# Low weight halves of an output product written by an accumulating transfer instead of a subtract

## The chip, the cores and the metric

The kernel runs on one core of a Trainium2 chip. Its time is the device time of one execution in microseconds (us). Engines: TensorE (PE, with its weight load PEld), VectorE (DVE), ScalarE (ACT), GpSimd (POOL) and SyncE (SP), each with its own instruction stream that runs in order; transfers are issued by an engine's queue and carried out by 16 DMA engines.

## The reference

Two layers of a transformer block over 256 tokens and 256 context tokens, model width 2048, branch width 4096, all float32. Layer 0 mixes tokens by a Fourier transform, layer 1 by windowed attention. Cut to what matters here:

```python
def _fourier_branch(h, w_in, w_mix):
    u, z = jnp.split(h @ w_in, 2, axis=-1)
    ...
    f = jnp.einsum('bngc,gcd->bngd', f, w_mix).reshape(b, n, D_BRANCH)
    return f * jax.nn.silu(z)

def reference(...):
    for i in range(DEPTH):
        ...
        x = x + gate * (y @ w_out[i])
        if need_ctx:
            xc = xc + gate_c * (yc @ w_out[i])
    return _rmsnorm(x, final_g)
```

The change touches `y @ w_out[0]` and `yc @ w_out[0]`, layer 0's output product.

## The kernel before, in words

**Precision.** [...] So every float32 operand is split in two fp32r tiles: a high half h (a rounded copy, ACT, L60) and a low half l = src - h (a subtract, DVE, L61). `mm3` (L72 to L75) forms a product with three matmuls, high times high (L73), high times low (L74) and low weights times high data (L75).

**Layout.** Both token sets lie side by side, 512 columns. A matmul has a 128x128 block of weights and 128x512 data. The branch result y is 32 tiles of 128x512 (`ys`), one for 128 branch channels.

**The changed loop** (L646 to L665) runs over 32 iterations i, in two sweeps `sw` of 1024 output channels each, so that the sweep's results fill the eight PSUM banks `o[0..7]`. In a sweep `kg` runs over 16 weight tiles of 128x2048 (1 MB). A weight tile holds two halves j of 128x1024, each for one tile of y, with eight blocks b of 128 output channels: 2 x 8 x 3 = 48 matmuls. `raw` (L43 to L47) loads a weight tile by SP's queue into one of three buffers, `ws_split` (L69) splits both halves (`half_split`, L63 to L67) into tiles of the pool `ws`, which has six buffers of 128x1024. `y_split0` (L624) splits the two y tiles of the next iteration into `act` tiles (34 buffers).

**What else runs there.** `ada_jobs` (L530 to L553) is a generator that computes layer 1's modulation vectors on DVE, from weight tiles of the same three `raw` buffers (`in_adw`), at about one tile an iteration; its lines are L545 (multiply and sum) and L535 (POOL loads `cb`). From kg = 12 on, POOL's queue loads two blocks of the input x each iteration (L656), into which `evac0` (L630 to L641) adds the gated result of each PSUM bank (L634, DVE) and sums squares (L637 ACT, L639 DVE) for the next norm, at kg = 15. In the first and the last kg of a sweep (`edge`) the matmuls go through the banks b on the outside and the halves j on the inside; else j is outside.

**Around it.** Ahead of the loop, the last of the z products ends: its result goes through a Silu on ACT into one of two z tiles (L583) and is multiplied into y on DVE (L584). The pools of that part are closed and their memory is used again. After the loop come transposes (L674, L680), the norm's sums (L691, which needs the last L639), then `rsqrt` (L81, L85) and a broadcast by L99, and layer 1's first product, whose weights are already being split (its `wl` subtracts stand among the last evacuations on DVE).

**Order.** The program is written in this order of lines, but a list scheduler decides the place of each instruction in its engine's stream from its own estimate of times; a tile pool with n buffers makes the write of use k wait for the last reader of use k - n.

The norm's sums after the loop:

```python
    for t in range(4):
        for i in range(2):
            PE.matmul(o[:, t : t + 1], sqs[i][:, t * P : (t + 1) * P], ones[:, 0:1], start=i == 0, stop=i == 1)   # L691
    r4 = rsqrt(const, o[:, 0:4], 4, "q")
```

## Time and profile before

| | |
|---|---|
| time, median of 3 runs | 1863.13 us (1860.94 to 1863.33) |
| the profiled execution | 1861.45 us |
| its span in the trace | 1859.1 us |
| mean granted TensorE clock | 0.995 of full |
| bytes read from HBM | 353.10 MB |
| DMA issues of the changed stage | `in_wo` 32 of 1024 KB, `in_adw` 64 of 1024 KB (some before it), `in_xT` 16 of 256 KB |

The profile lists, for the one profiled execution, busy times by engine, a chain of waits followed back from the last instruction, groups of instructions with the same line and tiles (busy time in all, mean in ns, idle time of the engine just before them and what ended it), and DMA issues with the time from issue to landing. A timeline row reads: start in us, duration, engine, line, operation, output tile <- input tiles, shapes, count, and in brackets the idle time before it with its releaser. Matmuls are pipelined, so a matmul's duration is longer than the distance between two starts. "PE ps L691 <- DVE act L639" reads: PE at line 691 waited for DVE's line 639 to write the tile.

### The profile page before, as it was taken

How to read it: one execution, taken by the hardware profiler on the slowest of the kernel's cores; microseconds unless marked ns; L12 is line 12 of the kernel's file. 1: busy time of each engine (PE TensorE's matmuls, PEld its weight loads, DVE VectorE, ACT ScalarE, POOL GpSimd, SP SyncE). 2: the span in 40 equal slices, each digit the busy share in tenths (PEclk: the TensorE clock that was granted, in tenths of full speed). 3: DMA queues.
4: the chain of work that ended last, by engine and by line, in shares of the span. 5: the costliest groups of instructions: out<-in, count | busy, mean ns of one | idle time of the engine just before them, and what ended most of it. 6: DMA issues, size and time to landing. Idle time of an engine off the chain costs nothing.

```text
span 1859.1 us, 26469 instructions
## 1 busy us (share of the span) xinstructions
PE 1817.6 (98%) x9889; PEld 1549.3 (83%) x9889; DVE 1389.6 (75%) x2766; ACT 954.6 (51%) x1657; POOL 176.8 (10%) x189
## 2 busy tenths in 40 slices
PE   6899999999999999999999999999999999999997
PEld 4579999888888888888888787888888888887886
DVE  4669888786868788687974825888878878887455
ACT  5444444432222243224322624888888888896343
POOL 0011111100000000000000001111220220300001
PEclk9899999999999999999999999999999999999999
DMA  9999888666656647763675323333333333434543
GB/s 395 407 296 246 246 220 242 228 226 244 224 212 234 227 172 264 264 236 131 226 286 204 114 92 143 128 136 126 124 115 135 136 115 135 159 137 179 186 178 136
DMA packets 76127, 367.39 MB, mean 198 GB/s; under 512 B 23200, under 2 KB 23344, under 8 KB 40928
## 3 DMA queue, kind: packets, MB, share of 16 engines
q1 hardware_dynamic: 49104, 324.83, 47.3%
q0 software_dynamic: 22320, 33.15, 7.1%
q10 hardware_dynamic: 4576, 7.74, 1.3%
q8 instruction: 77, 1.26, 0.3%
q14 instruction: 50, 0.41, 0.1%
HBM read 353.10 MB, written 12.59 MB: 197 GB/s over the span
## 4 chain that ended last, share of the span: by engine, by line
PE 90%; DMA 4%; DVE 3%; ACT 2%; issue 1%; POOL 0%; ACTq 0%; POOLq 0%; SPq 0%; DVEq 0%
PE ps L74 23%; PE ps L73 23%; PE ps L75 23%; PE ps L910 6%; PE ps L912 3%; DMA raw<-in_awp 3%; PE ps L966 3%; PE ps L981 2%; PE ps L980 2%; PE ps L946 2%; PE ps L947 2%; DMA raw<-in_wu 1%; PE ps L208 1%; PE ps L829 0%; DVE wl L61 0%
## 5 line engine op out<-in xcount | busy, mean ns | idle before, releaser
L60 ACT CAST wh<-raw 128x1024 fp32r<-128x1024 f32 x333 | 349.5, 1051 | 556.3 <-PE ps L74 483.5
L61 DVE TENSOR_TENSOR wl<-raw,wh 128x1024 fp32r<-128x1024 f32 x333 | 421.7, 1269 | 263.0 <-ACT wh L60 260.6
L74 PE MATMUL ps<-act,wh 128*128 128x512 f32 x1024 | 398.2, 389 | 0.0
L73 PE MATMUL ps<-act,wh 128*128 128x512 f32 x1024 | 393.6, 389 | 0.0
L75 PE MATMUL ps<-act,wl 128*128 128x512 f32 x1024 | 391.2, 389 | 0.0
L75 PEld LDWEIGHTS ps<-act,wl 128*128 128x128 f32 x1024 | 192.2, 188 | 39.9
L74 PEld LDWEIGHTS ps<-act,wh 128*128 128x128 f32 x1024 | 192.2, 188 | 39.8
L73 PEld LDWEIGHTS ps<-act,wh 128*128 128x128 f32 x1024 | 192.2, 188 | 39.8
L910 PE MATMUL ps<-h,wh 128*128 128x512 f32 x512 | 186.7, 400 | 0.0
L545 DVE CUSTOM_DVE_ANT_0 raw<-raw,cb 128x512 f32<-128x512 f32 x256 | 172.8, 689 | 14.5 <-DMA raw<-in_adw 10.6
L545 DVE CUSTOM_DVE_ANT_0 junk<-raw,cb 128x512 f32<-128x512 f32 x192 | 132.0, 687 | 10.8 <-ACT cb L537 8.3
L912 PE MATMUL ps<-h,wl 128*128 128x256 f32 x512 | 138.1, 280 | 0.0
L74 PE MATMUL ps<-wl,h 128*128 128x512 f32 x320 | 125.6, 392 | 1.5 <-DVE wl L61 1.5
L73 PE MATMUL ps<-wh,h 128*128 128x512 f32 x320 | 124.3, 397 | 0.2 <-ACT h L729 0.2
L75 PE MATMUL ps<-wh,h 128*128 128x512 f32 x320 | 124.4, 391 | 0.0
L910 PEld LDWEIGHTS ps<-h,wh 128*128 128x128 f32 x512 | 96.1, 188 | 18.7
L948 DVE CUSTOM_DVE_ANT_0 ps<-ps,mask,nsink 128x512 f32<-128x512 f32 x128 | 92.1, 754 | 11.8 <-PE ps L947 10.8
L951 ACT ACTIVATE p<-ps,mx 128x512 f32<-128x512 f32 x128 | 87.3, 687 | 24.6 <-DVE mx L948 24.0
L912 PEld LDWEIGHTS ps<-h,wl 128*128 128x128 f32 x512 | 96.8, 189 | 1.4
L61 DVE TENSOR_TENSOR pl<-ps,ph 128x512 fp32r<-128x512 f32 x128 | 83.7, 685 | 9.9 <-ACT ph L60 8.9
L956 ACT ACTIVATE p<-p,sm 128x512 f32<-128x512 f32 x128 | 85.4, 716 | 7.8 <-DVE sm L954 7.8
L74 PE MATMUL ps<-wl,ys 128*128 128x512 f32 x212 | 83.3, 393 | 0.0
(311 smaller groups left out, 3572.7 us busy)
## 6 DMA issues: line engine op xcount, KB each, us to landing
raw<-in_wz SPq DMA_DIRECT2D x64, 1024.0 KB, 4.9
raw<-in_adw SPq DMA_DIRECT2D x64, 1024.0 KB, 4.9
raw<-in_awp SPq DMA_DIRECT2D x32, 1024.0 KB, 13.8
raw<-in_wo SPq DMA_DIRECT2D x32, 1024.0 KB, 5.9
raw<-in_wq SPq DMA_DIRECT2D x32, 1024.0 KB, 4.8
raw<-in_wu SPq DMA_DIRECT2D x32, 1016.0 KB, 7.3
raw<-in_wo1b SPq DMA_DIRECT2D x16, 1024.0 KB, 4.9
act<-in_xT POOLq DMA_DIRECT2D x32, 256.0 KB, 5.6
```

Of the source, the lines that this page charges most:

```text
L60: S.copy(h, src)
L61: V.tensor_tensor(l, src, h.bitcast(F32), op=ALU.subtract)
L73: PE.matmul(o, wh, xh, start=start, stop=False)
L74: PE.matmul(o, wh, xl, start=False, stop=False)
L75: return PE.matmul(o, wl, xh, start=False, stop=stop).ins
L545: V.tensor_tensor_reduce(junk if s == 0 and i < 3 else wf, wf, cb[:, s, kq * 512 : kq * 512 + 512], 1.0, 0.0, ALU.mult, ALU.add, acc[:, i, ...
L910: PE.matmul(o[0], wh[:, q], hx1[k], start=k == 0, stop=k == KT - 1)
L912: PE.matmul(o[0][:, 0:N], wl[:, q], hx1[k][:, 0:N], start=False, stop=False)
L948: V.tensor_tensor_reduce(o, o, mask[:, tb, :], -0.125, nsink[:, i : i + 1], ALU.add, ALU.min, mx[:, tb : tb + 1])
L951: S.activation(pt[:, tb, :], so[tb], AF.Exp, bias=mx[:, tb : tb + 1], scale=-1.0, accum_out=sm[:, tb : tb + 1])
L956: S.activation(pt[:, tb, :], pt[:, tb, :], AF.Copy, scale=sm[:, tb : tb + 1])
L966: PE.transpose(o[:, (kt * 2 + tb) * P : (kt * 2 + tb + 1) * P], pt[:, tb, c : c + P], ident)
```

## The change

In each iteration the first half of the weight tile is split as before. For the second half ACT writes the high half h and, into a tile of a new pool `wx` with two buffers on the right side of memory, the negative of the same rounded value: the output type is fp32r too. Then POOL issues a transfer that reads the second half of the weights from HBM once more and adds it to that tile in place: l = -h + src, the same low half. The DVE subtract of that half is left out. The rest of the loop is as it was; a weight tile's low half of j = 1 now comes from `wx` instead of `ws`, which holds three new tiles an iteration instead of four.

```diff
+        wx = lay0.enter_context(tc.tile_pool(name="wx", reuse_waits="tile", bufs=2, side="right"))
         xin = []
...
-            w = ws_split(raw(a["wo0"][sw, kg]))
+            src = a["wo0"][sw, kg]
+            t = raw(src)
+            w = [half_split(t, 0)]
+            h = wsp.tile([P, 1024], F32R, tag="ws", name="wh")
+            l = wx.tile([P, 1024], F32R, tag="wx", name="wx")
+            S.copy(h, t[:, 1024:2048])
+            S.activation(l, t[:, 1024:2048], AF.Copy, scale=-1.0)
+            nc.gpsimd.dma_start(out=l, in_=src[:, 1024:2048], accum_op=ALU.add)
+            w.append((h, l))
```

In the changed file these are L643 (pool), L656 (high half), L657 (negated copy) and L658 (transfer). In the kernel before, the only transfers of this kind are those of layer 0's first product:

```python
            b = a["wu"][g, kh].rearrange("p (k s c) -> p k s c", k=8, s=2)[:, :, 1, :]
            nc.gpsimd.dma_start(out=v[:, :, 0, :], in_=b, accum_op=ALU.add)   # L133
```

## The prediction

> **What bounds the kernel now.** First I read the first page's totals and its chain of waits, then the groups, the engine's waits and 20 us windows of the changed stage.

> ```profile
> span 1859.1 us, 26469 instructions
> PE 1817.6 (98%) x9889; PEld 1549.3 (83%) x9889; DVE 1389.6 (75%) x2766; ACT 954.6 (51%) x1657; POOL 176.8 (10%) x189
> GB/s 395 407 296 246 246 220 242 228 226 244 224 212 234 227 172 264 264 236 131 226 286 204 114 92 143 128 136 126 124 115 135 136 115 135 159 137 179 186 178 136
> PE 90%; DMA 4%; DVE 3%; ACT 2%; issue 1%; POOL 0%; ACTq 0%; POOLq 0%; SPq 0%; DVEq 0%
> ```

> PE is busy for 98% of the span, and 90% of the chain that ends last is PE. The stage that is changed, layer 0's output product, runs from the second of these lines of PE's timeline to the third (the first ends the z product):

> ```profile
> 681.75 0.39 PE L75 MATMUL ps<-act,wl 128*128 128x512 f32 x1
> 681.98 0.39 PE L73 MATMUL ps<-act,wh 128*128 128x512 f32 x1
> ...
> 1029.91 0.39 PE L75 MATMUL ps<-act,wl 128*128 128x512 f32 x1
> ```

> It is 32 iterations of 48 matmuls, 1536 in 348.2 us: one starts every 0.2267 us, an iteration takes 10.88 us and starts at about 681.98 + 10.88 i. The waits of PE between 640 and 1100 us, and three windows of the stage (columns: length, busy time of PE, weight load, DVE, ACT, POOL, granted clock, share of the DMA engines, GB/s):

> ```profile
> PE ps L99 <- DVE qr L85: 2.1, 1, 2.1
> PE ps L73 <- ACT h L729: 0.2, 1, 0.2
> PE ps L691 <- DVE act L639: 0.2, 1, 0.2
> ...
> 680.00:700.00 20.00, 20.00 (x90) 16.57 (x89) 19.88 (x42) 9.02 (x14) 0.00 (x0) 1.00 0.43 159
> 800.00:820.00 20.00, 20.00 (x90) 16.55 (x89) 17.63 (x48) 4.22 (x4) 0.00 (x0) 1.00 0.70 258
> 1000.00:1020.00 20.00, 20.00 (x90) 16.57 (x89) 3.68 (x3) 3.94 (x4) 0.00 (x0) 1.00 0.29 103
> ```

> All three waits lie after the stage. Inside it PE never idles and has the full clock, although DVE is at 99% in the first window and 88% in the second. So the matmuls alone pace the stage; no work taken from DVE can shorten it, and only a late operand can move its end.

> **What is removed and added.** The groups of 657 to 1010 us:

> ```profile
> L61 DVE TENSOR_TENSOR wl<-raw,wh 128x1024 fp32r<-128x1024 f32 x66 | 80.7, 1224 | 55.5 <-ACT wh L60 55.3
> L60 ACT CAST wh<-raw 128x1024 fp32r<-128x1024 f32 x65 | 68.4, 1054 | 202.0 <-PE ps L74 147.6 <-DMA raw<-in_wo 47.7 <-DVE acc L545 4.2
> L656 POOL DMA_DIRECT2D act<-in_xT x16 | 8.6, 538 | 423.3 <-PE ps L75 423.1
> ```

> Removed: 32 subtracts, 32 x 1.224 = 39.2 us of DVE. Added: 32 negated copies of the same shape on ACT, by the row of L60 32 x 1.054 = 33.7 us, where ACT is busy 4 to 9 us of 20; and 32 POOL issues with 16.8 MB, or 512 KB in 10.88 us = 48 GB/s on windows that move 103 to 258. Matmuls are the same in number and order. All of this lies under PE, worth 0; if the cover were gone, ACT's 1.05 us per iteration would show as at most 33.7 us.

> **How long the new operand takes.** The only accumulating transfers of before are L133's, 508 KB each; beside them stand other loads:

> ```profile
> L133 POOL DMA_DIRECT2D raw<-in_wu x15: 1483/1491/1630, 116.3 to 307.5; - x15
> ...
> DMA to landing us min/median/max: 6.7/9.7/13.5
> ...
> raw<-in_wo SPq DMA_DIRECT2D x32, 1024.0 KB, 5.9
> act<-in_xT POOLq DMA_DIRECT2D x32, 256.0 KB, 5.6
> ```

> So 6.7 to 13.5 us bounds the landing, below too by a plain 256 KB at 5.6 (say 5). L133's rows came at 116 to 308 us, where the row of GB/s (40 slices of 46.5 us) shows 220 to 296; this stage moves 159 at its start. I take the low end, 6.7, since it is nearest in load.

> [...]

> **Steady state, 0.** The new pool has two buffers. A low half is overwritten by ACT once the last L75 of two iterations before has read it. In steady iterations its first use stands at place 26 of 48, so 22 matmuls of that iteration and the 48 of the next, plus the 4 or so by which its last use precedes the end, lie between release and first use: 74 x 0.2267 = 16.8 us. Ahead of the transfer ACT casts the high half, at most two y copies and the negated copy, 2.7 to 3.2 us with the issue's 0.54. That leaves 13.5 us, the largest landing of L133. In iterations 15 and 31, where halves alternate, first use is at place 6: 54 matmuls, 12.2 us, 9.1 to 9.8 left, against the median of 9.7. At 6.7 nothing stalls; a spread like L133's gives some tenths at the two edges, and I put 0.3.

> SP's loads move too. The raw slot of iteration n was freed by its second subtract; now the negated copy frees it, earlier in steady state, as no place on DVE is awaited. In the first iterations the loads start later than now, but what they bring is due a whole iteration, 10.9 us, later or more, and a load takes 5.9; 0. POOL's queue is in order: the new transfers stand behind L656's xT loads (which wait for PE), a cb load before i=8 and the mask load before i=29 (both wait for DVE's L545). The last of them:

> ```profile
> 990.97 0.53 POOL L56 DMA_DIRECT2D mask<-in_mask  x1 [3.06 <-DVE acc L545]
> ```

> It issues 12.4 us before iteration 29's operand is due at 1003.4, so a landing of up to 11 is covered; 0.

> **The first iteration, +4.1.** Here the pool has no history but its memory has: the first negated copy waits for DVE's L584 on the last z tile. DVE's and ACT's order of before at that place:

> ```profile
> 683.42 0.59 ACT L583 ACTIVATE z<-ps 128x512 f32<-128x512 f32 x1
> 683.91 1.65 ACT L60 CAST act<-y 128x512 fp32r<-128x512 f32 x3
> ...
> 685.34 1.29 DVE L61 TENSOR_TENSOR act<-y,act 128x512 fp32r<-128x512 f32 x2
> 686.54 1.22 DVE L61 TENSOR_TENSOR wl<-raw,wh 128x1024 fp32r<-128x1024 f32 x1
> 687.68 0.69 DVE L61 TENSOR_TENSOR act<-y,act 128x512 fp32r<-128x512 f32 x1
> 688.28 0.69 DVE L584 TENSOR_TENSOR y<-y,z 128x512 f32<-128x512 f32 x1
> ```

> In the changed order the second half's subtract and two y subtracts no longer stand ahead of L584: 1.15 + 2 x 0.6 us of starts earlier, so it ends at 688.97 - 2.35 = 686.6. ACT's z activation can start when the z product's last matmul is done (681.75 + 0.39, so about 682.3); then come a 1.06 us cast and five y copies of 0.55 (1.65 / 3): free at 686.6 as well. The negated copy ends at 687.7 and POOL issues; I take 688.0 for the start of the transfer. PE runs 40 matmuls of this iteration without it, since the edge order is kept but the scheduler puts the eight L75 of the second half in a block behind them: needed at 681.98 + 40 x 0.2267 = 691.05. At 6.7 us it lands at 694.7, so PE idles 3.7 us (at 5: 2.0; at 9.7: 6.7; at 13.5: 10.5). Behind the waiting matmul stands all of PE's queue, and the end moves by as much. The second transfer follows at once, due 10.88 us later, so it is not late again; but the negated copies also free two raw slots at that moment, and two 1 MB loads of SP's queue start beside it. That pulls towards the higher values.

> **Clock, +1.5.** The one place near by where PE runs thin:

> ```profile
> 1034.00:1036.00 2.00, 1.17 (x11) 1.09 (x10) 0.47 (x2) 1.55 (x4) 0.54 (x1) 1.00 0.88 246
> 1036.00:1038.00 2.00, 0.77 (x5) 0.80 (x6) 0.49 (x3) 0.00 (x0) 0.50 (x1) 0.92 0.92 259
> 1038.00:1040.00 2.00, 2.00 (x12) 2.00 (x11) 0.47 (x2) 0.82 (x2) 0.00 (x0) 0.50 0.99 382
> 1040.00:1042.00 2.00, 1.77 (x8) 1.18 (x7) 1.82 (x6) 2.00 (x5) 0.00 (x0) 0.73 1.05 396
> ```

> The granted clock falls to 0.50 after it and costs 2 x 0.50 + 2 x 0.27 = 1.5 us. A full stop of 3.7 us should do the same; of 2 us perhaps not, so 0 to 1.5. [...]

> **The tail, +1.1.** After the last matmul DVE evacuates:

> ```profile
> 1030.56 0.88 DVE L634 SCALAR_TENSOR_TENSOR act<-ps,gt,act 128x256 f32<-128x256 f32 x2
> 1031.34 1.23 DVE L61 TENSOR_TENSOR wl<-raw,wh 128x1024 fp32r<-128x1024 f32 x1
> 1032.47 0.70 DVE L639 TENSOR_TENSOR act<-act 128x512 f32<-128x512 f32 x1
> 1033.08 1.23 DVE L61 TENSOR_TENSOR wl<-raw,wh 128x1024 fp32r<-128x1024 f32 x1
> ...
> 1033.23 1.95 PE L691 MATMUL ps<-ones,act 128*128 128x1 f32 x16 [0.20 <-DVE act L639]
> 1037.23 1.64 PE L99 MATMUL ps<-ident,qr 128*128 128x128 f32 x8 [2.06 <-DVE qr L85]
> ```

> Today one subtract of the next weights stands before the last L639, on which L691 and then L99 wait; in the changed order two do, 1.23 less 0.1 of overlap: +1.1 (0 if DVE reaches one of them early).

> **Sum.** 3.7 + 1.5 + 0.3 + 1.1 = +6.6 on the profiled run's 1861.45 (span 1859.1 and 2.35 around it): 1868.1. The median of the runs is 1863.13, 1.7 higher, so 1869.7 by that; I say 1869. Ends for this case: 2.0 + 0 + 0 + 0, 1863.5, and 6.7 + 1.5 + 1.5 + 1.1 with late edges beginning, 1872.3. Some 0.2%, 3.7 us, is what a measurement of this kernel can tell from no change: below 1859.4 is faster, above 1866.9 slower.

> **Rivals.**
> A short landing, 0.20: at 4 to 5 us the first stall is 1.0 to 2.0, the clock holds, and with 0 to 1.1 for the tail the sum is 1.0 to 3.1: 1862.5 to 1864.6 from the profiled run, 1864 to 1866 from the median, not slower. For it: xT's 5.6 with half the bytes is mostly fixed time, and a plain 1 MB takes 5.9. Against: no accumulating row under 6.7. It decides below about 5.5 us, where first stall and tail stay under 3.7.
> Late edges, 0.13: at 13.5 us the first stall is 10.5, each edge 3.7 to 4.4, steady iterations just hold: 10.5 + 1.5 + 8 + 1.1 = 21.1, 1883. For it: L133's upper half, and DMA at 0.70 in the middle.
> Every iteration late, 0.07: a buffer's cycle is two iterations, so each us past 13.5 costs 0.5 us an iteration, 15 in all; 15 us gives 21.1 + 1.5 for the first + 3 for the edges + 22 = 47.6, 1909. For it: the transfer reads its target as well; against, L133's maximum under a fuller DMA.
> Faster, 0.05: DVE, relieved of 39 us, does the next weights' subtracts before the evacuation; then PE's idle 0.83 + 1.23 + 0.23 us in the four 2 us windows above and the 1.5 of clock could go, 3.8 at most: 1857.6, if the first landing is short too. Against: the tail's order has two subtracts, not none.
> The change doesn't do what it says, 0.03: DVE fills the freed time with the same L545 work earlier and the operand arrives in time everywhere; 1861 to 1864.

> **Chances.** The forecast has 0.52, of which 0.03 ends below 1866.9; slower is 0.49 + 0.13 + 0.07 = 0.69, faster 0.05, same 0.26. The range, 1862 to 1885, takes in the short landing and the late edges and leaves out the faster case, part of the last and the steady stalls, 0.17.

> **What would show it.** An idle time of PE of about 3.7 us near 691 released by a DMA of in_wo, and a clock of 0.50 in the 4 us behind it; no PE wait between 700 and 840 us; landings of the new transfers at 6 to 8 us; L691 about 1.1 us later behind the last matmul. It is wrong if the first gap is under 1 us, or if waits on the new tile recur every 10.88 us.

## The result, and the profile after

| | before | after |
|---|---|---|
| time, median | 1863.23 us | 1889.47 us (1888.67 to 1890.57) |
| ratio after / before, 95% interval | | 1.0137 (1.0116 to 1.0159) |
| span of the profiled execution | 1859.1 us | 1888.5 us |
| mean granted clock | 0.995 | 0.990 |

The change costs 26 us. The first page of after, span and busy totals:

```profile
span 1888.5 us, 26536 instructions
PE 1828.3 (97%) x9889; PEld 1554.1 (82%) x9889; DVE 1352.9 (72%) x2734; ACT 984.6 (52%) x1689; POOL 205.1 (11%) x221
```

DVE is 37 us less busy and ACT 30 us more, as the change says, and the span is 29.4 us longer. So the relief went to an engine that does not set the end, and something else was lost. The waits of PE between 600 and 1100 us (total, times, longest) say where to look first:

```profile
PE ps L75 <- DMA wx<-in_wo: 14.1, 3, 8.0
PE ps L99 <- DVE qr L85: 2.1, 1, 2.1
PE ps L700 <- DVE act L639: 1.2, 1, 1.2
```

A new wait holds 14.1 us, in three stalls and not in every iteration. PE's timeline shows the first matmul of the stage, the three matmuls that waited, the last of the stage and the first wait behind it:

```profile
685.54 0.39 PE L73 MATMUL ps<-act,wh 128*128 128x512 f32 x1
...
702.77 3.78 PE L75 MATMUL ps<-act,wx 128*128 128x512 f32 x8 [8.00 <-DMA wx<-in_wo]
...
792.68 0.50 PE L75 MATMUL ps<-act,wx 128*128 128x512 f32 x1 [2.22 <-DMA wx<-in_wo]
...
1029.08 0.50 PE L75 MATMUL ps<-act,wx 128*128 128x512 f32 x1 [3.86 <-DMA wx<-in_wo]
...
1057.59 0.40 PE L75 MATMUL ps<-act,wx 128*128 128x512 f32 x1
...
1061.89 1.97 PE L700 MATMUL ps<-ones,act 128*128 128x1 f32 x16 [1.17 <-DVE act L639]
```

From first to last matmul the stage takes 372.05 us instead of 347.93, 24.1 more. The waits are 14.1 of it. With each stall the granted clock falls, with the first already inside it (0.61 from 698 to 700 us). Windows of 2 us after the first, the second and the third (last columns: clock, DMA share, GB/s):

```profile
704.00:706.00 2.00, 2.00 (x6) 1.52 (x6) 0.00 (x0) 0.00 (x0) 0.00 (x0) 0.50 1.06 268
706.00:708.00 2.00, 2.00 (x6) 1.58 (x5) 1.92 (x5) 1.06 (x1) 0.06 (x1) 0.50 0.96 354
708.00:710.00 2.00, 2.00 (x9) 1.58 (x8) 1.97 (x8) 0.00 (x0) 0.79 (x1) 0.83 0.87 254
...
794.00:796.00 2.00, 2.00 (x7) 1.53 (x6) 1.97 (x7) 2.00 (x3) 0.89 (x1) 0.51 0.37 45
796.00:798.00 2.00, 2.00 (x7) 1.64 (x6) 1.97 (x6) 0.23 (x1) 0.00 (x0) 0.64 0.72 246
...
1030.00:1032.00 2.00, 2.00 (x6) 1.54 (x6) 0.00 (x0) 0.00 (x0) 0.00 (x0) 0.50 1.02 330
1032.00:1034.00 2.00, 2.00 (x9) 1.60 (x8) 0.00 (x0) 0.00 (x0) 0.00 (x0) 0.76 0.66 279
```

The part of full clock that is missing, times the time that PE works, gives 3.0 us behind the first stall (0.6 of it from 702.77 to 704, then 1.0, 1.0 and 0.34) and, counted in the same way, 1.7 behind each of the other two, 6.4 in all. The rest is in the matmuls themselves. Starts of the L75 in a first half, which uses `wl`, and in a second half, which uses `wx`, of one iteration without any wait:

```profile
944.75 0.39 PE L75 MATMUL ps<-act,wl 128*128 128x512 f32 x1
...
945.43 0.39 PE L75 MATMUL ps<-act,wl 128*128 128x512 f32 x1
...
948.16 0.40 PE L75 MATMUL ps<-act,wx 128*128 128x512 f32 x1
...
948.85 0.40 PE L75 MATMUL ps<-act,wx 128*128 128x512 f32 x1
...
952.32 0.40 PE L75 MATMUL ps<-act,wx 128*128 128x512 f32 x1
```

Three matmuls take 0.680 us (0.2267 each) in the first half; six groups of three from 948.16 to 952.32 take 0.693 us each. That is 13 ns for each of 256 uses of a `wx` block, 3.4 us in the stage. 14.1 + 6.4 + 3.4 = 23.9 of 24.1 us. From the stage's last matmul to layer 1's first it is 12.31 us (to 1069.90) instead of 10.90: 1.4 more.

The span grew by 3.6 us already ahead of the stage (685.54 against 681.98). There the instructions and their order on each engine are the same until some 5 us ahead of it; PE's waits before 660 us add up to 23.9 us in the profile of before and to 25 to 31 us in those of after and of all experiments, those that leave this change out among them, and the medians differ by 26 us where the two spans differ by 29. I take these 3.6 us for scatter of the start, not for a part of the change.

Why did the transfers come late? POOL's instructions around the first, the second and the third stall, and those of SP's queue around the first:

```profile
691.59 1.82 POOL L658 DMA_DIRECT2D wx<-in_wo  x2 [147.61 <-ACT wx L657]
...
780.06 0.55 POOL L535 DMA_DIRECT2D cb<-in_crow  x1 [14.41 <-DVE acc L545]
780.60 0.90 POOL L658 DMA_DIRECT2D wx<-in_wo  x1
...
1017.28 0.54 POOL L56 DMA_DIRECT2D mask<-in_mask  x1 [12.77 <-DVE acc L524]
...
1018.86 0.93 POOL L658 DMA_DIRECT2D wx<-in_wo  x1
```

```profile
690.83 0.33 SPq L46 DMA_DIRECT2D raw<-in_adw  x1
691.31 0.33 SPq L46 DMA_DIRECT2D raw<-in_wo  x1
692.26 11.94 SPq L46 DMA_DIRECT2D raw<-in_adw  x2
```

At the first stall two transfers of 512 KB start together with three loads of 1 MB, and the first lands 11.1 us after its issue. At the second and third the transfer had its operand (ACT's negated copies end at 775.97 and 1013.14) but stood behind the `cb` and the `mask` load, which wait for DVE. Landings of all 32, by the view of the tile:

```profile
DMA to landing us min/median/max: 5.2/9.1/14.2
```

### The profile page after: what moved, and what is told of

Its sections match the earlier page's. It is cut to its first block, busy times and chain, and to the rows that moved or that the text cites. A ratio compares the mean times of both kernels' runs of the same rounds, so it can differ in the third digit from the quotient of the medians.

```text
span 1888.5 us, 26536 instructions
## 1 busy us (share of the span) xinstructions
PE 1828.3 (97%) x9889; PEld 1554.1 (82%) x9889; DVE 1352.9 (72%) x2734; ACT 984.6 (52%) x1689; POOL 205.1 (11%) x221
## 4 chain that ended last, share of the span: by engine, by line
PE 68%; issue 16%; DMA 9%; DVE 5%; ACT 2%; POOL 0%; POOLq 0%; ACTq 0%; DVEq 0%; SPq 0%
PE ps L75 16%; PE ps L74 16%; PE ps L73 16%; PE ps L919 6%; PE ps L921 3%; DMA raw<-in_wu 3%; PE ps L975 3%; DMA raw<-in_awp 3%; DMA wx<-in_wo 2%; PE ps L990 2%; PE ps L989 2%; PE ps L955 1%; PE ps L956 1%; PE ps L208 1%; DVE wpl L61 1%
## 5 line engine op out<-in xcount | busy, mean ns | idle before, releaser
L60 ACT CAST wh<-raw 128x1024 fp32r<-128x1024 f32 x301 | 315.9, 1051 | 466.4 <-PE ps L74 375.5
L61 DVE TENSOR_TENSOR wl<-raw,wh 128x1024 fp32r<-128x1024 f32 x301 | 382.1, 1272 | 228.4 <-ACT wh L60 226.2
L74 PE MATMUL ps<-act,wh 128*128 128x512 f32 x1024 | 401.7, 392 | 0.0
L73 PE MATMUL ps<-act,wh 128*128 128x512 f32 x1024 | 396.0, 391 | 0.0
L75 PE MATMUL ps<-act,wl 128*128 128x512 f32 x768 | 295.9, 389 | 0.0
L73 PEld LDWEIGHTS ps<-act,wh 128*128 128x128 f32 x1024 | 194.5, 190 | 41.2
L74 PEld LDWEIGHTS ps<-act,wh 128*128 128x128 f32 x1024 | 193.2, 189 | 41.2
L545 DVE CUSTOM_DVE_ANT_0 raw<-raw,cb 128x512 f32<-128x512 f32 x256 | 172.7, 688 | 63.2 <-DMA raw<-in_adw 59.1
L75 PEld LDWEIGHTS ps<-act,wl 128*128 128x128 f32 x768 | 144.5, 188 | 30.1
L545 DVE CUSTOM_DVE_ANT_0 junk<-raw,cb 128x512 f32<-128x512 f32 x192 | 131.7, 686 | 47.0 <-DMA raw<-in_adw 31.3
L74 PE MATMUL ps<-wl,h 128*128 128x512 f32 x320 | 125.6, 392 | 1.5 <-DVE wl L61 1.5
L73 PE MATMUL ps<-wh,h 128*128 128x512 f32 x320 | 124.5, 397 | 0.2 <-ACT h L738 0.2
L75 PE MATMUL ps<-wh,h 128*128 128x512 f32 x320 | 124.2, 391 | 0.0
L75 PE MATMUL ps<-act,wx 128*128 128x512 f32 x256 | 103.4, 411 | 14.1 <-DMA wx<-in_wo 14.1
L61 DVE TENSOR_TENSOR pl<-ps,ph 128x512 fp32r<-128x512 f32 x128 | 83.6, 684 | 10.0 <-ACT ph L60 9.1
## 6 DMA issues: line engine op xcount, KB each, us to landing
raw<-in_wz SPq DMA_DIRECT2D x64, 1024.0 KB, 4.9
raw<-in_adw SPq DMA_DIRECT2D x64, 1024.0 KB, 6.4
raw<-in_awp SPq DMA_DIRECT2D x32, 1024.0 KB, 13.6
raw<-in_wo SPq DMA_DIRECT2D x32, 1024.0 KB, 6.9
raw<-in_wq SPq DMA_DIRECT2D x32, 1024.0 KB, 4.9
raw<-in_wo1b SPq DMA_DIRECT2D x16, 1024.0 KB, 4.8
```

Source lines behind the costliest of these rows:

```text
L60: S.copy(h, src)
L61: V.tensor_tensor(l, src, h.bitcast(F32), op=ALU.subtract)
L73: PE.matmul(o, wh, xh, start=start, stop=False)
L74: PE.matmul(o, wh, xl, start=False, stop=False)
L75: return PE.matmul(o, wl, xh, start=False, stop=stop).ins
L545: V.tensor_tensor_reduce(junk if s == 0 and i < 3 else wf, wf, cb[:, s, kq * 512 : kq * 512 + 512], 1.0, 0.0, ALU.mult, ALU.add, acc[:, i, ...
```

## The experiments

Each run lists its median and the ratio to the kernel before on the same chip with its 95% interval; the medians of before in these sessions lay between 1863.5 and 1866.3 us, single runs of it mostly between 1858 and 1871, so differences under 3 us are read from the profiles.

**The first operand, and POOL's queue.** Iteration 0 as before the change:

```diff
             w = [half_split(t, 0)]
+            if i == 0:
+                w.append(half_split(t, 1))
+            else:
...
```

> Iteration 0 splits both halves with ACT and DVE as before the change; iterations 1 to 31 are as changed. Theory (the first stall is the price of a new pool whose first operand is issued 6 us into the stage): its 8.0 us of PE idle and the 3.0 us of half clock behind it go, the stalls near 792 and 1029 us stay: 1889.5 - 11 = 1878.5 us. Rival (the traffic of the transfers is late anyway and the first stall only moves to iteration 1 or 2): 1885 us or more, with a wait of over 3 us on a wx tile before 730 us.

Measured: 1877.86 us, 1.0065 (1.0039 to 1.009). No stall before 730 us; four small ones remain, the longest 2.5:

```profile
PE ps L75 <- DMA wx<-in_wo: 5.6, 4, 2.5
```

The 11 us of the first stall are confirmed as the price of the first iteration, and it did not move on. The next edit orders POOL's queue:

```diff
-                with tc.issue_after(hs_end[2]):
+                with tc.issue_after(wx_in[-2] if wx_in else hs_end[2]):
                     nc.gpsimd.dma_start(cb, ...)
...
+    with tc.issue_after(wx_in[-1]):
         rope = cload("rope", [P, 2, 2, 64], pool=l1c)
         mask = cload("mask", [P, 2, 512], pool=l1c)
         sink = cload("sink", [P, 64], pool=l1c)
```

> As changed, but on POOL's queue the last cb load stands behind the transfer of iteration 8, and rope, mask and sink behind the transfer of iteration 31. Theory (the second and third stall come from standing behind those loads, which wait for DVE): PE's waits of 2.2 and 3.9 us and the half clock behind them, 1.7 and 1.6 us, go, the first stall stays: 1889.5 - 9.4 = 1880 us. Rival (the DMA engines are full and the transfers land late wherever they are queued): 1887 us or more, with PE waits on wx tiles near 792 and 1029 us of over 2 us.

Measured: 1879.46 us, 1.0068 (1.0046 to 1.009). One stall is left, the first:

```profile
PE ps L75 <- DMA wx<-in_wo: 8.1, 1, 8.1
```

The second and third stall were waits in POOL's queue, though the DMA engines were as full as in after (share 0.92 in 720 to 780 us). Both edits together:

> Both edits together: iteration 0 keeps its subtract, and cb, rope, mask and sink stand behind transfers on POOL's queue. Theory (the two causes add up): all three stalls are gone, 1877.9 + 1879.5 - 1889.5 = 1868 us, 1867 to 1871. Rival (with accumulating transfers taking the DMA engines to 0.9 of their time, loads are late and a wait of over 2 us shows in another iteration): 1873 us or more.

Measured: 1869.2 us, 1.0021 (1.001 to 1.0033), and 0.5 us of waits on `wx` in all. The two causes add up and are all the stalls there are. The 4.1 us that are left over the kernel before on the same chip (1865.09 us) are about the slower matmuls and the tail (3.4 and 1.4).

**What adding costs.** The same transfer without `accum_op`:

```diff
-            nc.gpsimd.dma_start(out=l, in_=src[:, 1024:2048], accum_op=ALU.add)
+            nc.gpsimd.dma_start(out=l, in_=src[:, 1024:2048])
```

> The transfer only copies and does not add, so the low halves of the second halves hold the weights themselves and the output differs; bytes, places and waits are the same. Theory (adding in the transfer takes the DMA engines about twice the time of copying, 3.0 us of all 16 for 512 KB against 1.4): landings of wx fall from a median of 9.1 to about 6 us, the DMA share of steady windows from 0.9 to about 0.75, the first stall from 8.0 to 3 to 5 us, and the time to 1875 to 1883 us. Rival (the landing is set by the loads that run beside it and by the queue, not by the adding): landings of 8.5 us or more, first stall of 7 us or more, 1887 us or more.

Measured: 1876.13 us, 1.0058 (1.0038 to 1.0077); landings 3.9/7.8/11.6 us, the first stall 6.5 us, no other. The DMA view of 905 to 960 us has one row for POOL's queue, first of after, then of this run (packets, MB, share of 16 engines):

```profile
q0 software_dynamic: 837, 3.08, 29.9%
```

```profile
q0 software_dynamic: 720, 2.62, 13.1%
```

29.9% of 55 us for 3.08 MB are 5.3 us per MB, 13.1% for 2.62 MB are 2.8: an accumulating transfer of 0.52 MB takes all sixteen engines for 2.8 us, a copy for 1.4. That half of the theory held, and the time lies in its range. But the landings fell only to 7.8 us in the median where about 6 was expected, and the first stall from 8.0 to 6.5 where 3 to 5 was: adding is 1.5 us of the first stall, not the bulk of it. What the rest is, a run shows that holds the three loads back:

```diff
+            if i == 0:
+                hold = [nc.sync.dma_start(held, l[:, 0:1].bitcast(F32)).ins]
...
+            with tc.issue_after(hold[0]) if i == 2 else nullcontext():
+                t = raw(src)
...
+            with tc.issue_after(hold[0]) if i in (1, 2) else nullcontext():
+                for _ in range(ada_rate.get(i, 1)):
+                    next(ada)
```

> As changed, with one small transfer more on SP's queue, out of the first wx tile: it waits until the first accumulating transfer has landed, and the three 1 MB loads that were issued at 690.8 to 692.3 us stand behind it. Theory (the first transfer lands after 11.1 us and not after 6.7 because three 1 MB loads share the DMA engines with it; transfers of the same kind without a load beside them land in 5.2 to 5.8): it lands in 5.5 to 8 us, the first stall falls from 8.0 to 2.5 to 5 us, the time from 1889.5 to 1881 to 1886 us. Rival (the first landing is slow for a reason of its own, the second accumulating transfer behind it or a cold start of POOL's queue): 10 us or more, first stall of 7 us or more, 1888 us or more.

Measured: 1889.9 us, 1.0121 (1.0104 to 1.0138). POOL, SP's queue and PE at the start:

```profile
691.15 1.82 POOL L660 DMA_DIRECT2D wx<-in_wo  x2 [147.61 <-ACT wx L659]
```

```profile
696.80 0.33 SPq L663 DMA_DIRECT2D held<-wx  x1
697.22 0.38 SPq L46 DMA_DIRECT2D raw<-in_adw  x1
```

```profile
696.83 3.60 PE L75 MATMUL ps<-act,wx 128*128 128x512 f32 x8 [2.50 <-DMA wx<-in_wo]
```

With no load beside it, and only the second transfer of its kind, the first transfer lands in 5.6 us (691.15 to 696.8) and the stall is 2.5. Both are as the theory had them, so the first landing was late by contention with the loads. The expected gain in time did not come, and by the time alone the rival would have won: the held loads are late in turn (two waits for ACT's `wh`, 1.9 us) and the later stalls add up to more, four of 8.3 us on `wx` against two of 6.1 in after. I read this as one transfer taking from the next what the first was given, with the DMA engines at 0.89 of their time from 700 to 760 us in after; no run shows that link by itself.

**Without the transfer.** The negated copy alone:

```diff
-            nc.gpsimd.dma_start(out=l, in_=src[:, 1024:2048], accum_op=ALU.add)
```

> The changed kernel without the transfer: the low halves of the second halves stay the negated high halves, so the output differs. Theory (all the stalls are waits for the transfers; ACT's 34 us and the relief of DVE by 39 us cost and bring nothing): no PE wait on wx over 0.3 us, and what is left over the kernel before is the slower matmuls on wx (3.4 us) and the tail (1.4 us): 1864.3 + 4.8, 1868 to 1871 us. Rival (the negated copies come late on ACT, so that part of the stalls is ACT's): waits of PE on ACT's wx of 2 us or more in the first iteration, 1873 us or more.

Measured: 1870.12 us, 1.0025 (1.0012 to 1.0037), with no wait on `wx`. ACT's extra 34 us are hidden and DVE's 39 us bring nothing. The opposite, the traffic without a reader (both halves split as before the change, the copies and transfers beside them):

```diff
-            w = [half_split(t, 0)]
-            h = wsp.tile([P, 1024], F32R, tag="ws", name="wh")
+            w = ws_split(t)
             l = wx.tile([P, 1024], F32R, tag="wx", name="wx")
-            S.copy(h, t[:, 1024:2048])
...
-            w.append((h, l))
```

> Both halves are split by ACT and DVE as before the change, and the negated copies and accumulating transfers run beside them into wx tiles that nothing reads. Theory (a transfer costs PE only where PE waits for its result; the traffic beside it is hidden): no stall over 0.5 us, 1864.3 + 0 to 2 us. Rival (the doubled DMA time of the transfers delays the weight loads themselves): waits of PE that go back to raw loads, 1868 us or more.

Measured: 1880.64 us, 1.0087 (1.0068 to 1.0106), against the theory:

```profile
PE ps L73 <- ACT wh L60: 4.3, 7, 1.3
PE ps L75 <- DVE wl L61: 3.2, 6, 0.5
PE ps L73 <- DVE act L634: 1.9, 3, 1.1
```

Here PE waits for its ordinary weights, and three times for an evacuation. So the traffic is not free when nothing waits for its result. Two ways are possible: the loads themselves are slower, or the added copies hold ACT and the raw slots, since a negated copy also waits until an older transfer has left its `wx` tile. ACT's waits from 680 to 1060 us speak for the loads:

```profile
ACT wh L60 <- DMA raw<-in_wo: 106.5, 16, 11.6
ACT wx L655 <- DMA raw<-in_wo: 67.2, 12, 10.0
```

That is 174 us of waiting for loads of `in_wo`, where before had 47.7 us; ACT waited for an older transfer only once, for 3.8 us, and SP's queue for a negated copy once, for 19.7. By the page the loads of `in_wo` land in 7.0 us in the median against 5.9, those of `in_adw` in 5.7 against 4.9. No run has the copies without the transfers and with both splits, so the share of the copies stays open.

**The slower matmuls.** DVE's subtract, written into the `wx` tile:

```diff
-            S.activation(l, t[:, 1024:2048], AF.Copy, scale=-1.0)
-            nc.gpsimd.dma_start(out=l, in_=src[:, 1024:2048], accum_op=ALU.add)
+            V.tensor_tensor(l, t[:, 1024:2048], h.bitcast(F32), op=ALU.subtract)
```

> No transfer and no negated copy: DVE subtracts the second half as before the change, but into the wx tile. Theory (the 0.2311 us between matmuls of a half that uses wx, against 0.2267, comes from where the tile lies or how its pool waits): the spacing stays at 0.231 in second halves, PE has no wait inside the stage, 1863.2 + 3.4 + 1 = 1867.5 us. Rival (it comes from the transfer or from what it writes): spacing 0.2267 everywhere, 1863 to 1865 us.

Measured: 1870.93 us, 1.0033 (1.002 to 1.0046), some 2 us over the theory's time on this chip. The groups of 920 to 960 us (behind the bar: busy time, mean of one in ns, idle time):

```profile
L75 PE MATMUL ps<-act,wx 128*128 128x512 f32 x30 | 11.9, 397 | 0.0
L75 PE MATMUL ps<-act,wl 128*128 128x512 f32 x29 | 11.3, 389 | 0.0
```

No transfer, and the matmuls on `wx` are still slower. The same with the tiles 832 bytes lower:

```diff
-        wx = lay0.enter_context(tc.tile_pool(name="wx", reuse_waits="tile", bufs=2, side="right"))
+        wxs = ExitStack()
+        wx = wxs.enter_context(tc.tile_pool(name="wx", reuse_waits="tile", bufs=2))
...
+        wxs.close()
```

> As e4_subtract_into_wx, but the two wx tiles lie 832 bytes lower in each partition's memory: they begin 160 bytes past a multiple of 512, on the right side 480 (the tiles of ws, with 0.2267 us, 96). Theory (the place within 512 bytes sets the weight load's speed): 0.2267 us between matmuls in all halves, 3.4 us less than e4_subtract_into_wx in the stage, 1867.5 us. Rival (the upper end of the memory is slower, or the pool's kind is): 0.231 us as in e4_subtract_into_wx, 1871 us.

Measured: 1869.16 us, 1.0032 (1.0016 to 1.0048), 397 against 389 ns again. Moving the tiles from 480 to 160 bytes past a multiple of 512 does not help, against the theory. So the kernel before was tried with its weights in other places, each an edit of where a pool lies; first the upper end, then the two other orders of the pools raw, ws, act:

```diff
-    wsp = ctx.enter_context(tc.tile_pool(name="ws", bufs=6))
+    wsp = ctx.enter_context(tc.tile_pool(name="ws", bufs=6, side="right"))
```

```diff
+    wsp = ctx.enter_context(tc.tile_pool(name="ws", bufs=6))
     rawp = ctx.enter_context(tc.tile_pool(name="raw", bufs=3))
-    wsp = ctx.enter_context(tc.tile_pool(name="ws", bufs=6))
     actp = ctx.enter_context(tc.tile_pool(name="act", bufs=34))
```

```diff
-    rawp = ctx.enter_context(tc.tile_pool(name="raw", bufs=3))
-    wsp = ctx.enter_context(tc.tile_pool(name="ws", bufs=6))
     actp = ctx.enter_context(tc.tile_pool(name="act", bufs=34))
+    wsp = ctx.enter_context(tc.tile_pool(name="ws", bufs=6))
+    rawp = ctx.enter_context(tc.tile_pool(name="raw", bufs=3))
```

> The kernel before the change with one edit: all six buffers of the pool ws lie at the upper end of each partition's memory, where the wx tiles lie, instead of below the act tiles; nothing else moves but the other pools' addresses. Theory (weights at the upper end are read more slowly, some 13 ns a matmul): in the stage all three matmuls of a group slow down, 0.240 us between matmuls instead of 0.2267, the stage 20 us longer and the kernel 1890 us or more. Rival (the slower matmuls come from the wx pool's kind, not from its place): 0.2267 us, 1863 to 1867 us.

> The kernel before the change with the pools raw and ws in the other order, so that the weights lie 24576 bytes lower in each partition (from 21600 instead of 46176). Theory (a matmul takes longer the higher its weights lie, about 5.6 ns for the 158592 bytes of e15_weights_at_upper_end): 0.2258 us between matmuls, 1.4 us less in the stage and up to 6 us less in the kernel: 1858 to 1862 us. Rival (only places past some height are slower): 0.2267 us as now, 1862 to 1866 us.

> The kernel before the change with the pools in the order act, ws, raw: the act tiles, which hold the moving data, lie lowest (from 21600), the weights at 91232 to 115808. Theory (longer the higher the weights lie): 45056 bytes higher, 0.2283 us, 2.4 us more in the stage, 1866 to 1872 us. Rival (only places past some height are slower): 0.2267 us, 1862 to 1866 us.

Measured: 1886.44 us, 1.0131 (1.0111 to 1.0151) for the upper end (204768 to 229344); 1863.13 us, 0.9999 (0.9988 to 1.0011) for the lowest place; 1864.82 us, 1.0005 (0.9994 to 1.0015) for the middle. The window from 800 to 1000 us, in which PE has no wait, of before, of the upper end, of the lowest and of the middle (x is the number of matmuls):

```profile
800.00:1000.00 200.00, 200.00 (x885) 165.58 (x884) 160.63 (x375) 59.74 (x75) 5.89 (x11) 1.00 0.61 229
```

```profile
800.00:1000.00 200.00, 200.00 (x863) 162.14 (x862) 161.56 (x377) 58.95 (x75) 4.83 (x9) 1.00 0.59 217
```

```profile
800.00:1000.00 200.00, 200.00 (x884) 165.70 (x883) 160.56 (x375) 59.79 (x75) 5.89 (x11) 1.00 0.61 230
```

```profile
800.00:1000.00 200.00, 200.00 (x884) 165.73 (x883) 164.83 (x388) 59.74 (x75) 6.97 (x13) 1.00 0.61 228
```

863 against 885 matmuls in the same time: weights at the upper end cost 2.5%. Between 21600 and 116000 bytes the three places tried do not differ, so nothing is gained by the lower one. The size was expected too high (0.240 us; 200 / 863 is 0.232): when all weights lie there a matmul loses 5 to 6 ns, not 13. A group of three thus loses 17 ns with all its weights at the upper end and 13 with one, so the loss is not a fixed price for each weight block; why is open. Nor is height told apart from the place within 512 bytes: all places without a loss (21600, 46176, 91232) begin 96 bytes past a multiple of 512, the slow ones 480 or 160, and no run has a tile at the upper end with 96. That the place matters is shown; by which of the two, and where the slow part begins, is not.

**The tail.** As e6_first_and_queue, with the first weights of layer 1 split behind the last L639:

```diff
-                w = ws_split(raw(a["wkv"][kg]))
+                t = raw(a["wkv"][kg])
+                with tc.issue_after(sq_end[0]) if kg < 2 else nullcontext():
+                    w = ws_split(t)
```

> As e6_first_and_queue, but the first two weight tiles of layer 1's first product are split behind the last L639 on DVE. Theory (the tail's 1.4 us come from two subtracts ahead of the last L639): PE's wait for L639 falls from 1.2 to 0.2 us or less and the stretch from the last matmul of the stage to layer 1's first from 12.3 to about 10.9 us: 1869.2 - 1.4 = 1867.8 us. Rival (the first product then waits for its own low weights, or the tail is set by the norm's chain): the stretch stays at 12 us or more, 1869 us or more.

Measured: 1869.71 us, 1.0034 (1.0023 to 1.0046), not told apart from e6_first_and_queue in time. In the profile the wait for L639 is gone and the stretch from the first transpose behind the stage to layer 1's first matmul is 10.55 us (10.67 before, 12.07 after, 12.78 in e6_first_and_queue), though DVE's `qr` comes later:

```profile
PE ps L99 <- DVE qr L85: 2.7, 1, 2.7
```

The cause of the tail is shown in place; that it is worth its 1.4 us in the whole kernel is not.

No version beat the kernel before.

## Why the prediction was wrong, point by point

The direction was right, the size was not: 1869 us with a range to 1885 was forecast, 1889.5 measured. Two terms of the sum failed: the landing of the first transfer, 6.7 us for a measured 11.1, and the zero for POOL's queue, which held two transfers for stalls of 2.2 and 3.9 us. Step by step:

| step | predicted | measured |
|---|---|---|
| the matmuls pace the stage, DVE's relief is worth | 0 | 0 (e5: no wait, no gain) |
| first transfer issued, from the stage's start | 6.0 us | 6.05 us |
| its landing | 6.7 us | 11.1 us |
| first stall | 3.7 us | 8.0 us |
| steady iterations | 0 | 0 |
| iterations 15 and 31 | 0.3 us | 0 |
| POOL's queue | 0 | 2.2 + 3.9 us |
| half clock | 1.5 us | 3.0 + 1.7 + 1.7 us |
| place of the new tiles | not in the sum | 3.4 us |
| tail | 1.1 us | 1.4 us |

**The step that failed first** is the one that took the low end of L133's landings, 6.7 us, "since it is nearest in load". The load of a 20 us window is the wrong measure: the negated copies that start the transfer free the raw slots too, so the transfer meets its own competition in the same microsecond. The prediction named two 1 MB loads and then left them without a price. The old trace had one: 13.30 MB of loads in 63.5% of 905 to 960 us, 2.6 us of all engines per MB. By the same view in after it is 2.8 us (11.59 MB in 59.8%), so the three loads that came are 9 us, and two accumulating transfers are 5.6; 14.6 us together, and the second transfer landed after 14.2. With the loads away it was 5.6 us, below the low end taken.

**The second** is the zero for POOL's queue. The transfer of iteration 29 was said to be covered because the mask load "issues 12.4 us before" it is due, by the old trace. But that load waits for DVE's last sum (L524), which waits for the last `in_adw` load, and these loads land later now (by the page in 6.4 us in the median, 4.9 before). DVE's group of L545 in the stage, before and after (last: idle time and what ended it):

```profile
L545 DVE CUSTOM_DVE_ANT_0 raw<-raw,cb 128x512 f32<-128x512 f32 x149 | 99.0, 689 | 12.2 <-DMA raw<-in_adw 10.6
```

```profile
L545 DVE CUSTOM_DVE_ANT_0 raw<-raw,cb 128x512 f32<-128x512 f32 x152 | 101.1, 688 | 61.0 <-DMA raw<-in_adw 59.1
```

DVE waited 59.1 us for those loads where it had waited 10.6. Part of that is only the relief, which brings DVE to the loads earlier: in e5_no_transfer, which has the relief and no transfer, the wait is 31.9 us. In stage time the mask load came at 331.7 us (1017.28 - 685.54) instead of 309.0 (990.97 - 681.98). Of the 22.7 us, 14.9 are the first two stalls with their half clock (8.0 + 3.0 + 2.2 + 1.7) and some 3.1 the slower matmuls of 29 iterations; the 4.7 that remain are less than the loads cost. In e5_no_transfer, where the stage begins at 687.62, the mask load came earlier than in before, at 303.5 us (991.16 - 687.62):

```profile
991.16 0.54 POOL L56 DMA_DIRECT2D mask<-in_mask  x1 [5.42 <-DVE acc L524]
```

Against this the transfers made it 28.2 us later: 14.9 by the stalls, and the 13.3 left over I put down to late loads. The same holds for `cb` in iteration 8, for which no row was priced at all. What is behind a wait on another engine moves when that engine's inputs move.

**The third** is the clock. That a full stop of that length halves it was right (0.50 behind 8.0 and 3.9 us); the fall lasted longer behind 8.0 us (10.24 us, to 708.69), and it came behind 2.2 us as well (0.51 from 794 to 796 us), which the prediction held for doubtful. That was its author's estimate; none of its rows shows a stop of 2 us at which the clock held. Its own rows of before could have made it less so: the longest stop in the place where the clock fell to 0.50 is the 2.06 us of L99, though PE ran thin around it as well. What the runs show of the clock is in the last section.

**Not seen** was the place of the new pool. The prediction says "Matmuls are the same in number and order", which was so; that each could take longer because of where its weights lie (863 instead of 885 in 200 us in e15_weights_at_upper_end) was in no row of before, where all of this stage's weights lie in one place.

**The tail** had mechanism and size right: 1.0 us more of PE's wait for L639. The rest is in the clock behind it, which the term left out, and that part does not go with the tail's order: half clock there lasted 3.41 us in before (to 1041.09) and 6.83 in after (to 1070.51), but layer 1's first matmul (L73) took 0.50 us in e5_no_transfer, which has the late tail, the length at full clock behind a wait (792.68 in after), and 0.79 in e16_weights_lowest, which has the old one, against 0.62 in before and 0.77 in after.

Three of the prediction's figures do not come out of its own rows, and nothing hangs on them: with two y copies of 0.55 us ACT's work ahead of a transfer is 3.7 us and not 3.2, which leaves 13.1 us in steady iterations; 12.2 less 2.7 to 3.2 is 9.0 to 9.5, not 9.1 to 9.8; and the cases named as outside the range have 0.15 at most, not 0.17.

Of the rivals, the late edges had nearly the right sum (1883) by a landing of 13.5 us and a first stall of 10.5, but iterations 15 and 31 never waited; the stalls came where POOL's queue was held, at iterations 8 and 29, so that its sum came near is luck. "Every iteration late" did not happen: PE has no wait from 800 to 1000 us, with a median landing of 9.1 and 13.5 to spend. The short landing, a transfer of 4 to 5 us, was not reached by any of the 32, the least being 5.2; of the plain copies of e3_plain_transfer the fastest took 3.9.

## What to carry to other kernels

An operand that is moved from a busy engine to a transfer must be priced at the moment at which it is issued: list what the same release lets start, add up the time that all of it takes on the DMA engines (an accumulating one counts twice here, 2.8 against 1.4 us for 512 KB), and follow each instruction ahead of it in its queue to what that one waits for. Where PE has no idle time in a stage, as here, relief of another engine is worth nothing (e5_no_transfer: 39 us off DVE, 1870.12 us), and a buffer that is moved in memory is a change of its own (13 ns for each group of three matmuls with one of its weights in `wx`).

## What the runs showed of the hardware that was not expected

```profile
782.23 0.96 PE L75 MATMUL ps<-act,wx 128*128 128x512 f32 x3 [2.46 <-DMA wx<-in_wo]
...
1015.12 0.50 PE L75 MATMUL ps<-act,wx 128*128 128x512 f32 x1 [2.11 <-DMA wx<-in_wo]
```

```profile
784.00:786.00 2.00, 2.00 (x10) 1.67 (x9) 1.97 (x6) 1.51 (x3) 0.89 (x1) 1.00 0.53 90
...
1016.00:1018.00 2.00, 2.00 (x7) 1.52 (x6) 0.00 (x0) 0.00 (x0) 0.00 (x0) 0.51 1.01 326
```

- An accumulating transfer takes the DMA engines twice the time of a copy of the same bytes, 2.8 against 1.4 us of all sixteen for 512 KB (after and e3_plain_transfer, 905 to 960 us).
